# Ten places instead of five for the row sums of layer 1's shift and scale in a two-layer diffusion step

## The chip, the core and the metric

The kernel runs on one core of a Trainium2 chip. Five engines work side by side, each through its own queue in order: TensorE (PE) multiplies matrices, VectorE (DVE), ScalarE (ACT) and GpSimd (POOL) work on elements, SyncE (SP) starts transfers. An instruction that needs another engine's result waits, and everything behind it on its engine waits too. The metric is the device time of one execution in microseconds (us).

## What is computed

The reference is one step of a two-layer trunk over 512 latent and 128 context tokens of width 1024. Layer 0 is gated attention with 16 query heads in 4 groups, layer 1 a gated linear recurrence. In front of each layer the tokens are scaled and shifted by two vectors that come from a condition vector:

```python
def _adaln(cond, w, b):
    mod = jax.nn.silu(cond.astype(jnp.float32)) @ w.astype(jnp.float32) + b.astype(jnp.float32)
    mod = mod.astype(cond.dtype)
    return jnp.split(mod, 3, axis=-1)
...
for i in range(DEPTH):
    sh_p, sc_p, g_p = _adaln(c_ctx, ada_w[i], ada_b[i])
    sh_s, sc_s, g_s = _adaln(c, ada_w[i], ada_b[i])
    hp = xp * (1.0 + sc_p) + sh_p
    hs = xs * (1.0 + sc_s) + sh_s
    # layer 0: attention over 640 keys (latent) or 128 keys (context); layer 1: recurrence
    xp = _layer_norm(DEEPNORM_ALPHA * xp + g_p * out_p, ln_gain[i], ln_bias[i])
    xs = _layer_norm(DEEPNORM_ALPHA * xs + g_s * out_s, ln_gain[i], ln_bias[i])
```

Layer 1's shift and scale (sh and sc for i = 1) are needed only when layer 0 is done, and are worked out while its attention runs.

## The kernel before

**Attention and side work.** Layer 0's attention is a main thread of steps (`att_gen`), one tuple of steps for each of 32 sample units and 4 prompt units. A sample unit is one head with 256 queries. Its steps are two fronts (scores `sc` on PE, row maximum `nm` on DVE, exponential `p` on ACT, reciprocal `rc` on DVE, scaling of `p` on POOL), three transpositions (`pt` on PE, copied to `pts` by ACT, or by DVE for the short last one) and, for each pair of units, the product with the values (`pot` on PE) that DVE multiplies into `gs`. The scores use two PSUM double banks in turn.

A side thread (`Side`) is stepped between the attention's steps. It holds, in this order: the query chunks 1, 2 and 3 (`q_gen`), the splitting of the output weights `attn_w_out` (`wo_gen`: ACT casts to `wohi`, DVE subtracts to `wolo`) and the splitting of `gs` into `hhi` (ACT) and `hlo` (POOL). The string `SIDE_AT` says how many side steps follow each attention step. Where a front of query chunk c is due, `side.until` runs whatever is left of that chunk on the spot.

**A query chunk.** `q_gen` multiplies 640 tokens by 256 columns in three units of 2, 2 and 1 token tiles, 24 products (`qmm`) a tile in two steps of 12. After a unit come sums of squares (`sq`, `ss`), rotation (`u`, `r`), scaling (`qn`), the split (`qs`) and transpositions (`qps`) into `X`, which the scores read. Between those steps `q_gen` takes one step of a filler at the places that `FILL_AT` names: a digit for the unit's first tile, a letter for the step (a to d are the product steps, e stands behind the rotation). Whatever of the filler is left by the chunk's end runs there, one step after another. For chunks 1 and 2 the filler works out gate vectors on PE.

**The row sums.** For chunk 3 the filler is `cols_gen`: five jobs, each a 128x1024 piece of layer 1's weights (`in_ada_c`, 512 KB, loaded by SP into one of three `raw` buffers). A job has two row sums, one for each condition vector: DVE multiplies the piece by the vector (`silb`, spread over all partitions) and adds up along the row, with the products themselves written to a throwaway tile `spill` (line 361). The trace shows each as one SCALAR_TENSOR_TENSOR and one DVE_READ_ACCUMULATOR. So there are ten filler steps. Behind the last, DVE adds the bias (`shsc`, line 365), from which `modA` and `modB` are made (lines 1144 to 1146), and POOL issues two transfers of layer 0's gate into the buffer that held `silb` (line 341). The other 11 of the 16 jobs ran earlier.

**What sets the order.** The first half of the program, up to the end of attention, is written in the order of these steps and then reordered by a scheduler with a model of each engine's time (`tc.block(schedule_with_timeline_sim=True)`); instructions that are pinned keep their order among themselves. The second half follows its own plan and is not touched.

Of the kernel before, what the change touches and what calls it, by code (L numbers as in the profile page):

```python
# [34 lines left out]
HALVES = ((0, 320), (320, 640))  # L35
HALF_PIECES = (slice(0, 512), slice(512, 1024))
RAW_AHEAD = 2
FILL_AT = {1: '0b0e2e', 2: '0b0e2e4e', 3: '0a0b0e2e4e'}
LEAD = (1, 1)
RAW_START = 8  # L40
EARLY = 2
# [3 lines left out]
SIDE_T = 2.2  # L45
SIDE_AT = (
    "0100021120010100020100012001210201010101000002111001021000000130"
    "2002020010001200011201020101300010100102000000201112120001100001"
    "3100002000111000000310010102010113001000012000120300210000012")
RES_AT = 6  # L50
SEVEN = range(1, RH - 1)
# [103 lines left out]
def hybrid_step(ctx: ExitStack, tc: tile.TileContext, a: dict, o: dict):  # L155
# [589 lines left out]
    def q_gen(c, X, fill):  # L745

        w = Weights("attn_w_in", c, (nc.vector, nc.vector), tuple(last_split))
        yield
        spots = {FILL_AT[c][i:i + 2] for i in range(0, len(FILL_AT[c]), 2)}
        pend = None  # L750
# [1338 lines left out]
```

## Time and profile before

| | us |
|---|---|
| median of three runs | 818.72 |
| lowest, highest | 817.18, 822.82 |
| the profiled execution, its own time | 818.12 |
| its span, first to last instruction | 816.3 |
| granted TensorE clock, mean | 0.993 |
| query chunk 3's products on PE | 233 to 269 |
| end of attention, start of the output product | 324.5 |

Times inside the span are counted from its start. A row of the chain of waits gives start, length, engine, tile and line of a piece of the path that ended last. A row of the timeline gives start, length, engine, line and operation, and in square brackets how long the engine had stood idle and for whom. Where instructions of an engine are pipelined, their lengths overlap, and the distance between starts is what one costs.

### The profile page before, as it was taken

To read this page: it belongs to the slowest core of one execution; us is meant where nothing else is said; L and a number is where in the kernel's file an instruction comes from. 1 tells how busy PE (TensorE), PEld (TensorE's weight loads), DVE (VectorE), ACT (ScalarE), POOL (GpSimd) and SP (SyncE) were. 2 spreads that over 40 slices of the span, in tenths; PEclk is the share of its full clock that TensorE was granted. 3 is DMA by queue.
4 is the path that set the end of the run, shared out by engine and by line. 5 is a ranking of instruction groups with operands and counts; after the bars stand their busy time and mean duration, and the time that the engine had idled before them with its cause. 6 is when DMAs were issued, how large, how long until landed. Compare 5 with 4: busy or idle time off the path is not lost.

```text
span 816.3 us, 19278 instructions
## 1 busy us (share of the span) xinstructions
PE 791.5 (97%) x7953; PEld 700.9 (86%) x7953; DVE 598.5 (73%) x1083; ACT 451.3 (55%) x894; POOL 217.1 (27%) x261
## 2 busy tenths in 40 slices
PE   8999999999999989999999999999999999999994
PEld 6779999878888766888999999998999999998873
DVE  4567767686578885676799777868786876788376
ACT  2252545566565786232565766747484856667342
POOL 0124001353434853010600224122140414131211
PEclk9999999999999999999999999999999999999998
DMA  9944343224140060631531342325242344232442
GB/s 325 395 160 159 104 155 132 104 96 165 52 130 28 27 206 7 238 118 49 143 105 53 98 120 71 111 64 128 66 122 85 98 108 144 92 106 74 142 149 77
DMA packets 36630, 98.12 MB, mean 120 GB/s; under 512 B 5296, under 2 KB 12480, under 8 KB 36544
## 3 DMA queue, kind: packets, MB, share of 16 engines
q1 hardware_dynamic: 25872, 78.95, 28.9%
q0 software_dynamic: 4768, 14.18, 6.0%
q10 hardware_dynamic: 5904, 3.78, 1.5%
q8 instruction: 62, 1.02, 0.5%
q14 instruction: 24, 0.20, 0.1%
HBM read 86.06 MB, written 10.83 MB: 119 GB/s over the span
## 4 chain that ended last, share of the span: by engine, by line
PE 82%; DVE 8%; ACT 4%; DMA 2%; issue 2%; POOL 2%; SPq 0%; ACTq 0%; DVEq 0%; POOLq 0%
PE vgps L1383 8%; PE vgps L1379 4%; PE pot L950 4%; PE pt L1036 4%; PE rps L1451 4%; PE outp L1213 3%; PE outp L1215 3%; PE outp L1214 3%; PE rps L1405 3%; PE rps L1407 3%; PE rps L1453 3%; PE rps L1406 3%; PE rps L1452 3%; PE acc L568 3%; PE sc L923 2%; PE lv L1682 2%
## 5 line engine op out<-in xcount | busy, mean ns | idle before, releaser
L1029 POOL TENSOR_SCALAR p<-p,rc 128x640 f32<-128x640 f32 x64 | 57.1, 898 | 114.8 <-DVE rc L1028 97.6
L1720 POOL COPY At<-near 32x160 f32<-32x160 f32 x32 | 15.6, 489 | 197.0 <-PE lv L1688 196.0
L1023 ACT ACTIVATE p<-sc,nm 128x640 f32<-128x640 f32 x64 | 51.2, 802 | 24.9 <-DVE nm L1018 15.7
L1018 DVE TENSOR_REDUCE nm<-sc 128x1 f32<-128x640 f32 x64 | 51.7, 816 | 13.0 <-PE sc L924 12.8
L1405 PE MATMUL rps<-h1hi,rw 128*128 128x320 f32 x176 | 55.4, 315 | 0.0
L1407 PE MATMUL rps<-h1hi,rw 128*128 128x320 f32 x176 | 54.5, 310 | 0.1
L1406 PE MATMUL rps<-h1lo,rw 128*128 128x320 f32 x176 | 54.4, 309 | 0.0
L1036 PE MATMUL pt<-small,p 128*128 128x128 f32 x320 | 49.0, 277 | 2.8 <-DVE pts L928 1.2
L1383 PE MATMUL vgps<-rw,h1hi 128*128 128x512 f32 x180 | 48.3, 393 | 0.0
L1036 PEld LDWEIGHTS pt<-small,p 128*128 128x128 f32 x320 | 36.5, 140 | 11.6 <-issue 5.7
L1655 ACT COPY kc<-A 128x640 f32<-128x640 f32 x48 | 38.3, 797 | 12.2 <-DVE A L1706 11.5
L928 ACT COPY pts<-pt 128x512 f32<-128x512 f32 x64 | 36.1, 590 | 15.3 <-PE pt L1036 15.2
L923 PE MATMUL sc<-kk,X 128*128 128x320 f32 x128 | 42.3, 340 | 1.7 <-ACT p L1023 1.6
L1726 ACT COPY At<-lv 32x160 f32<-32x160 f32 (+1 forms) x48 | 15.9, 330 | 45.9 <-PE lv L1688 45.5
L950 PE MATMUL pot<-pts,vv 128*64 128x256 f32 x320 | 38.3, 384 | 2.1 <-DVE pts L928 2.0
L380 PE MATMUL gps<-hhi,whi 128*128 128x320 f32 x128 | 40.0, 312 | 0.1
L381 PE MATMUL gps<-hlo,whi 128*128 128x320 f32 x128 | 39.6, 309 | 0.0
L382 PE MATMUL gps<-hhi,wlo 128*128 128x320 f32 x128 | 39.5, 309 | 0.0
L1383 PEld LDWEIGHTS vgps<-rw,h1hi 128*128 128x128 f32 x180 | 33.1, 188 | 6.7
L924 PE MATMUL sc<-klo,X 128*128 128x320 f32 x128 | 38.5, 310 | 0.0
L1383 PE MATMUL vgps<-wspare,h1hi 128*128 128x512 f32 x140 | 38.2, 394 | 0.0
L1711 DVE TENSOR_TENSOR A<-A,T 128x640 f32<-128x640 f32 x32 | 27.2, 850 | 10.9 <-PE lv L1682 10.8
(347 smaller groups left out, 2633.9 us busy)
## 6 DMA issues: line engine op xcount, KB each, us to landing
raw<-in_rec_w_in SPq DMA_DIRECT2D x40, 512.0 KB, 3.7
raw<-in_ada_m SPq DMA_DIRECT2D x16, 512.0 KB, 8.1
raw<-in_attn_w_in SPq DMA_DIRECT2D x16, 512.0 KB, 5.2
raw<-in_ada_s SPq DMA_DIRECT2D x16, 512.0 KB, 3.7
adaraw<-in_ada_c SPq DMA_DIRECT2D x11, 512.0 KB, 5.5
raw<-in_attn_w_out SPq DMA_DIRECT2D x8, 512.0 KB, 3.8
raw<-in_rec_w_out SPq DMA_DIRECT2D x8, 512.0 KB, 3.6
raw<-in_ada_c SPq DMA_DIRECT2D x5, 512.0 KB, 4.4
```

What stands on the lines that cost most here:

```text
L380: nc.tensor.matmul(ps[:, :320], w.hi(k)[:, c], hhi[:, k, t], start=(k == 0), stop=False)
L381: nc.tensor.matmul(ps[:, :320], w.hi(k)[:, c], hlo[:, k, t], start=False, stop=False)
L923: nc.tensor.matmul(out, X[:, h, t0:t0 + P], kk[:, c, k0:k1], start=True, stop=False)
L950: nc.tensor.matmul(pot[j * HD:(j + 1) * HD, :CW], vv[:, slot, c * HD:(c + 1) * HD], moving[j], start=first, stop=last)
L1018: nc.vector.tensor_reduce(nm[:, 0:1], sc[:, :, :320], AX.XY, ALU.max, negate=True)
L1023: return nc.scalar.activation(halves(p[:]), sc[:, :, :320], AF.Exp, bias=nm[:, 0:1], accum_out=su[:, 0:1])
L1029: nc.gpsimd.tensor_scalar(p, p, rs[:, 0:1], 1.0, ALU.mult, ALU.mult)
L1036: nc.tensor.transpose(pt[:, i * 256 + q * P:i * 256 + (q + 1) * P], ps[q][:, (k0 + i) * P:(k0 + i + 1) * P], ident)
L1383: nc.tensor.matmul(out, h1hi[:, k, t], wvg[i][:, k % 4].rearrange("p e n -> p (e n)"), start=(k == 0), stop=(k == KT - 1))
L1405: nc.tensor.matmul(ps[:, j, :320], hi[:, k, :], h1hi[:, k, t], start=(k == 0), stop=False)
L1406: nc.tensor.matmul(ps[:, j, :320], hi[:, k, :], h1lo[:, k, t], start=False, stop=False)
L1407: nc.tensor.matmul(ps[:, j, :320], lo[:, k, :], h1hi[:, k, t], start=False, stop=(k == KT - 1))
```

## The change

Two constants. `FILL_AT` names ten places in chunk 3 instead of five: behind three of the first unit's four product steps, three of the second's four, one of the third's two, and, as before, behind the rotation of each of the three units. `SIDE_AT` gets six more side steps, in the attention steps in which the chunk's products stand, so that the products keep about their place although there are more steps among them.

```diff
-FILL_AT = {1: '0b0e2e', 2: '0b0e2e4e', 3: '0a0b0e2e4e'}
+FILL_AT = {1: '0b0e2e', 2: '0b0e2e4e', 3: '0a0b0c0e2a2b2d2e4a4e'}
...
 SIDE_AT = (
     "0100021120010100020100012001210201010101000002111001021000000130"
-    "2002020010001200011201020101300010100102000000201112120001100001"
+    "2002020010001200011201020101301010110102010010201112120101101001"
     "3100002000111000000310010102010113001000012000120300210000012")
```

In written order, before, row sums 1 to 3 stand in the first unit, 4 after the second, 5 after the third, and 6 to 10 at the end of the chunk; 7 to 10, with the chunk's last transposition behind them, run in one go where `side.until` forces the rest out. Now 1 to 4 stand in the first unit, 5 to 8 in the second and 9 and 10 in the third, nothing is forced out, and the first split of `attn_w_out` comes three attention steps earlier. No instruction is added or removed on any engine. SP issues the same transfers in the same order.

The scheduler then makes of it the following. DVE, around the rotation of chunk 3's first unit (`r`, `qn`, `qs`), before:

```order
L673 TENSOR_TENSOR qn<-r,rstd 128x512
L955 TENSOR_TENSOR gs<-pot,gs 128x256
L928 COPY pts<-pt 128x256
L361 SCALAR_TENSOR_TENSOR spill,shsc_80<-raw,silb 128x1024
L1028 RECIPROCAL rc<-su 128x1
L976 TENSOR_REDUCE nmp<-pscp 128x4
L726 TENSOR_TENSOR qs_3169<-qn,qs_3169 128x8x64
```

One row sum, the fourth, stood here. Now, on DVE at the same place:

```order
L955 TENSOR_TENSOR gs<-pot,gs 128x256
L673 TENSOR_TENSOR qn<-r,rstd 128x512
L361 SCALAR_TENSOR_TENSOR spill,shsc_80<-raw,silb 128x1024
L928 COPY pts<-pt 128x256
L726 TENSOR_TENSOR qs_3153<-qn,qs_3153 128x8x64
L361 SCALAR_TENSOR_TENSOR spill,shsc_80<-raw,silb 128x1024 x2
L1018 TENSOR_REDUCE nm<-sc 128x1
L928 COPY pts<-pt 128x256
L361 SCALAR_TENSOR_TENSOR spill,shsc_80<-raw,silb 128x1024
L1028 RECIPROCAL rc<-su 128x1
L976 TENSOR_REDUCE nmp<-pscp 128x4
```

Four row sums, the fifth to the eighth, stand here with four short operations between them; the fourth has moved ahead of this place.

DVE at the end of chunk 3, where the last split `qs` and the splits of the output weights `wolo` stand, before:

```order
L361 SCALAR_TENSOR_TENSOR spill,shsc_80<-raw,silb 128x1024
L928 COPY pts<-pt 128x256
L1018 TENSOR_REDUCE nm<-sc 128x1
L726 TENSOR_TENSOR qs_3551<-qn,qs_3551 128x4x64
L361 SCALAR_TENSOR_TENSOR spill,shsc_80<-raw,silb 128x1024
L1028 RECIPROCAL rc<-su 128x1 x2
L361 SCALAR_TENSOR_TENSOR spill,shsc_80<-raw,silb 128x1024
L1018 TENSOR_REDUCE nm<-sc 128x1
L361 SCALAR_TENSOR_TENSOR spill,shsc_80<-raw,silb 128x1024 x2
L1018 TENSOR_REDUCE nm<-sc 128x1
```

Five row sums, the last of the ten. Now, on DVE around the last split:

```order
L673 TENSOR_TENSOR qn<-r,rstd 128x256
L1018 TENSOR_REDUCE nm<-sc 128x1
L1028 RECIPROCAL rc<-su 128x1
L726 TENSOR_TENSOR qs_3565<-qn,qs_3565 128x4x64
L1018 TENSOR_REDUCE nm<-sc 128x1
L1028 RECIPROCAL rc<-su 128x1
L928 COPY pts<-pt 128x256
L1018 TENSOR_REDUCE nm<-sc 128x1
L264 TENSOR_TENSOR wolo<-raw,wohi 128x1024 x2
```

None is left there; the bias and `modA`, `modB` have gone with them to a place ahead of the third unit's rotation.

POOL, from the splitting of `gs` on, before:

```order
L1161 TENSOR_TENSOR hlo<-gs,hhi 128x640 x4
L213 TENSOR_TENSOR rstd<-rs_t,mhalf 128x4
L1029 TENSOR_SCALAR p<-p,rc 128x640 x3
L1161 TENSOR_TENSOR hlo<-gs,hhi 128x640
L1029 TENSOR_SCALAR p<-p,rc 128x640 x3
L341 DMA gate_3606<-gated_102 128x1024 x2
L1029 TENSOR_SCALAR p<-p,rc 128x640 x6
```

The two gate transfers stood behind ten scalings and splits. Now, on POOL:

```order
L1161 TENSOR_TENSOR hlo<-gs,hhi 128x640 x3
L341 DMA gate_3571<-gated_102 128x1024
L1029 TENSOR_SCALAR p<-p,rc 128x640
L341 DMA gate_3571<-gated_102 128x1024
L1161 TENSOR_TENSOR hlo<-gs,hhi 128x640
L1029 TENSOR_SCALAR p<-p,rc 128x640
L213 TENSOR_TENSOR rstd<-rs_t,mhalf 128x4
```

They are issued among the first splits, one by one, ahead of the scalings that they stood behind.

## The prediction

> **What bounds the kernel now.** I read the page first: how long the span is and which engine fills it.
>
> ```profile
> span 816.3 us, 19278 instructions
> PE 791.5 (97%) x7953; PEld 700.9 (86%) x7953; DVE 598.5 (73%) x1083; ACT 451.3 (55%) x894; POOL 217.1 (27%) x261
> ```
>
> TensorE is busy 97% of the span and the change takes no product away. So only time in which PE stands or runs below its pace can be won. The change touches the attention from about 228 to 324.5 us, so I cut that into stretches (columns: length, then busy time and count of PE, PEld, DVE, ACT, POOL, then granted clock, DMA share, GB/s).
>
> ```profile
> 228.00:278.15 50.15, 49.33 (x410) 42.89 (x409) 38.30 (x82) 34.18 (x77) 26.54 (x28) 1.00 0.21 64
> 278.15:295.14 16.99, 12.23 (x88) 9.17 (x86) 16.97 (x34) 12.73 (x27) 12.15 (x10) 1.00 0.51 160
> 295.14:324.50 29.36, 28.05 (x219) 20.66 (x219) 18.66 (x40) 20.75 (x49) 12.14 (x14) 1.00 0.21 70
> ```
>
> In the second stretch PE falls to 12.23 of 16.99 us, and DVE is busy for 16.97: DVE is the bound there, and nowhere else nearby. The chain of waits says with what (start, length, engine, tile, line):
>
> ```profile
> 276.30 1.24 PE pt L1036 x10
> ...
> 279.07 1.20 DVE spill L361
> ...
> 285.74 1.06 DVE spill L361
> 286.82 1.74 DVE spill L361 x3
> ...
> 291.20 0.64 DVE wolo L264
> ...
> 295.14 0.98 PE pt L1036 x7
> ```
>
> The path leaves PE behind 276.30 and is back at 295.14. Between, it runs through row sums and what stood behind them on DVE. How much of the stretch is lost? Its PE work, grouped, and what the same instructions cost where PE runs without waits:
>
> ```profile
> L1036 PE MATMUL pt<-small,p 128*128 128x128 f32 x40 | 6.5, 280 | 2.5 <-DVE pts L928 1.2 <-POOL p L1029 0.7 <-ACT pts L928 0.5
> L923 PE MATMUL sc<-kk,X 128*128 128x320 f32 x12 | 4.2, 356 | 0.8 <-ACT p L1023 0.8
> L924 PE MATMUL sc<-klo,X 128*128 128x320 f32 x12 | 3.6, 308 | 0.0
> L950 PE MATMUL pot<-pts,vv 128*64 128x256 f32 x20 | 2.4, 384 | 1.5 <-DVE pts L928 1.5
> L734 PE MATMUL qps<-identr,qs 128*128 128x128 f32 x4 | 0.5, 238 | 0.0
> ```
> ```profile
> 230.06 0.87 PE pt L1036 x8
> 234.25 0.12 PE qmm L391
> 297.87 2.31 PE pot L950 x20
> 300.77 0.15 PE sc L923
> 300.92 0.14 PE sc L924
> ```
>
> A transposition costs 0.87/8 = 0.109 us, a score 0.145, twenty value products 2.31. The stretch's work is 44 x 0.109 + 24 x 0.145 + 2.31 = 10.6 us. It took 16.99, so 6.4 us are lost: the most that this change can win here.
>
> **The change part by part: what leaves the end of the chunk.** Five row sums leave the stretch, with the bias and the two modulation vectors.
>
> ```profile
> L361 DVE SCALAR_TENSOR_TENSOR spill<-raw,silb 128x1024 f32<-128x1024 f32 x5 | 7.2, 1458 | 0.0
> L365 DVE TENSOR_TENSOR shsc<-shsc,small 128x16 f32<-128x16 f32 x1 | 0.6, 594 | 0.0
> L1029 POOL TENSOR_SCALAR p<-p,rc 128x640 f32<-128x640 f32 x7 | 9.0, 1289 | 3.4 <-DVE modB L1146 3.4
> L341 POOL DMA_DIRECT2D gate<-gated x2 | 1.2, 602 | 1.4 <-DVE spill L361 1.4
> L1023 ACT ACTIVATE p<-sc,nm 128x640 f32<-128x640 f32 x7 | 5.6, 801 | 2.0 <-DVE nm L1018 1.1 <-DVE rc L1028 0.9
> L736 ACT CAST X<-qps 128x512 fp32r<-128x512 f32 x1 | 0.6, 587 | 1.8 <-PE qps L734 1.8
> ```
>
> DVE drops from 16.97 by 7.2 + 0.6 and about 0.8 of small ones to some 8.4 us, below PE's 10.6. POOL loses the 1.4 us wait for the last row sum and its scalings should fall back from 1289 ns towards the 859 of the rows below: 12.15 - 7 x 0.43 - 1.2 = 8 us. What is late next is ACT: 12.73 us of work that stays (exponentials, copies, the casts of the output weights). If it works without a gap, the stretch takes 12.7 us and the gain is 16.99 - 12.73 = 4.3. The ends: at PE's pace, with ACT's surplus worked off in the next stretch (20.75 of 29.36 us busy), 6.4; if only the 2.0 us that ACT idles for DVE (1.1 and 0.9) come back, 2.0. I take 4.3, the row of the engine that is next.
>
> **What arrives among the products.** In this place the first stretch's rows price the work:
>
> ```profile
> L361 DVE SCALAR_TENSOR_TENSOR spill<-raw,silb 128x1024 f32<-128x1024 f32 x5 | 6.0, 1218 | 1.2 <-DMA raw<-in_ada_c 1.2
> L1018 DVE TENSOR_REDUCE nm<-sc 128x1 f32<-128x640 f32 x17 | 13.7, 818 | 5.5 <-PE sc L924 5.4
> L928 DVE COPY pts<-pt 128x256 f32<-128x256 f32 x9 | 3.8, 417 | 1.2 <-PE pt L1036 1.2
> L673 DVE TENSOR_TENSOR qn<-r,rstd 128x512 f32<-128x512 f32 x2 | 1.8, 892 | 0.1
> L1029 POOL TENSOR_SCALAR p<-p,rc 128x640 f32<-128x640 f32 x16 | 13.6, 859 | 18.5 <-DVE rc L1028 13.0 <-PE pt L1036 5.0 <-PE pot L950 0.4
> 247.90 2.38 PE L950 MATMUL pot<-pts,vv 128*64 128x256 f32 x20
> 251.59 0.41 DVE L955 TENSOR_TENSOR gs<-pot,gs 128x256 f32<-128x256 f32 x1
> 254.06 0.92 DVE L726 TENSOR_TENSOR qs<-qn,qs 128x512 fp32r<-128x512 f32 x1
> 246.69 0.41 PE L923 MATMUL sc<-kk,X 128*128 128x320 f32 x1 [0.68 <-ACT p L1023]
> ```
>
> DVE's load rises from 38.3 to about 38.3 + 5 x 1.3 + 1.1 = 45.9 of 50.15 us: it fits, barely. Row sums 5 to 8 stand in a bunch there, so I count from the end of one value product to the next. DVE: gs 0.41, qn 0.89, a row sum 1.22 and its read 0.08, pts 0.42, qs 0.92, two row sums 2.60, nm 0.82, pts 0.42 = 7.8 us, and this second `pts` is what the next value product waits for. PE has 48 products, 20 transpositions, 4 long scores and 8 short ones in between: 48 x 0.12 + 20 x 0.109 + 4 x 0.145 + 8 x 0.109 = 9.4 us. That cover leaves 1.6. But DVE was late there already: pot ended at 250.28, gs began at 251.59, so 1.3 is gone and 0.3 remains. The scaling behind the fourth row sum is due 2.4 us later than it is ready by the same count. So the cost is between 0 and, should all four row sums lie on the path, 4 x 1.30 = 5.2. The nearest row of a wait here is PE's 0.68 for a score that stood behind DVE and ACT; I take one such, 0.7, because the count comes out near zero.
>
> **Costed at nothing.** Row sums 9 and 10 stand in front of the third unit's products, and 4 moves up by one row sum's length; without cover each would cost 1.3. The transfers of the pieces keep their order on SP; a piece needs a buffer that an earlier row sum freed, and these now come earlier, so I expect no wait longer than the 1.2 that stands in the row above. The loads of the output weights start earlier for the same reason. POOL's two gate issues (1.2 us) move ahead of scalings, but behind splits that POOL does anyway. The first `wohi` and `wolo` come three attention steps earlier; DVE has room there now. Behind 324.5 the program is the same, only shifted.
>
> Sum: -4.3 + 0.7 = -3.6 us. The profiled execution took 818.1 (span 816.3 and 1.8 around it), which gives 814.5; it lies 0.6 under the median of 818.7, against which I forecast **815.1**.
>
> **A rule weighed.** POOL's scaling took 1289 ns on average where five row sums ran and 859 where they were rarer; a row sum took 1458 against 1218. Stretching thus adds 0.24 to a row sum. The Trainium skill, SBUF — State Buffer, "Who interferes with whom", says that a VectorE instruction with two SBUF inputs contends with a GpSimd one that reads SBUF, through a port that both share; a row sum is such an instruction. The trace agrees with the direction. By its exclusive form, where the loser waits for the other's whole instruction, each of four could wait up to 0.86 for a scaling, 3.4 together, which makes the last rival below the dearer one: the sum would be -0.9.
>
> **The rivals.**
> *Half comes back.* The row sums go, but ACT keeps its waits for others: X waited 1.8 us for PE. Then 2.0 return less 0.7: 817.4. For it: ACT's row names DVE for only 2.0. Against: qps itself stood behind DVE's late qs.
> *PE's full pace.* All 6.4 return and the bunch is free: 812.3. Against: ACT's 12.73 is more than 10.6.
> *The bunch decides; the row sums do not lie one by one.* The scheduler has put four of them between two value products. From 0.3 us of further lateness on, each microsecond of DVE is one of PE. With row sums as in the crowded row, 3 x 0.24 = 0.7 more, it costs 0.4, which I have covered; with all four on the path, 5.2 against 4.3: 819.6, slower than before. Against: 48 products as cover, and PE's order holds them there.
>
> **How the numbers follow.** The forecast, 813.5 to 816.5, gets 0.58; half, up to 819, 0.20; full pace 0.10; the bunch 0.12. The range runs from full pace to the bunch, 812.0 to 820.0, rounded outward, and leaves under 2 in 10 outside. About 1%, 8.2 us, is what a measurement of this kernel can tell from no change. The whole loss is 6.4, so faster by over 1% gets 0.02; slower by over 1% would need more than every moved row sum on the path: 0.02; within 1% 0.96.
>
> **What would show it.** Right: DVE's share in the stretch behind the last products falls to about two thirds, no spill in the chain there, PE's share back above nine tenths, the attention ends near 321. Wrong: waits of the value product or of transpositions for `pts` and `rc` around 250 to 262, row sums over 1.5 us there, or ACT with idle time for PE in the old place.

## The result, and the profile after

The changed kernel took 824.98 us (median of 8 runs, 822.61 to 826.87) beside 819.06 us for the kernel before (8 runs, 817.18 to 822.82). The ratio is 1.0064, with a 95% interval of 1.0048 to 1.0081: slower by some 5.3 us by the ratio, where 3.6 us less was forecast. The profiled execution took 826.87 us, the slowest of the eight, while that of the kernel before, at 818.12, lies below its median; the parts read below therefore hold more loss than 5.3 us. Its page begins:

```profile
span 825.1 us, 19288 instructions
PE 793.6 (96%) x7953; PEld 701.5 (85%) x7953; DVE 605.8 (73%) x1083; ACT 450.2 (55%) x894; POOL 215.1 (26%) x261
```

The first question is in which part of the program the time came. The instructions of one tile, grouped by line, give the first and the last start of each line. Two of these rows enclose the attention: its first score product, and the first product of the output projection behind it. The kernel before, and then the changed one:

```profile
L923 PE MATMUL sc<-kk,X x128: 302/309/417, 130.8 to 316.1; 128*128 128x320 f32 x128
L1213 PE MATMUL outp<-wohi,hhi x80: 389/389/504, 324.6 to 382.7; 128*128 128x512 f32 x80
```
```profile
L923 PE MATMUL sc<-kk,X x128: 302/310/636, 131.4 to 323.6; 128*128 128x320 f32 x128
L1213 PE MATMUL outp<-wohi,hhi x80: 388/390/502, 332.9 to 391.1; 128*128 128x512 f32 x80
```

From first score to output projection it was 324.6 - 130.8 = 193.8 us, and it is now 332.9 - 131.4 = 201.5. Behind it 816.3 - 324.6 = 491.7 us were left, and now 825.1 - 332.9 = 492.2. So the loss lies inside the attention. Nor is it spread out there (columns as in the prediction's windows):

```profile
248.00:256.00 8.00, 8.00 (x70) 7.21 (x66) 7.96 (x18) 3.06 (x7) 4.76 (x3) 1.00 0.03 10
256.00:264.00 8.00, 8.00 (x70) 6.86 (x69) 7.43 (x15) 5.40 (x16) 3.75 (x3) 1.00 0.36 124
264.00:272.00 8.00, 7.64 (x63) 6.15 (x61) 7.97 (x14) 7.32 (x16) 4.28 (x3) 1.00 0.17 52
272.00:280.00 8.00, 2.79 (x20) 2.30 (x20) 7.93 (x10) 0.59 (x1) 7.35 (x8) 0.90 0.39 145
280.00:288.00 8.00, 6.90 (x32) 5.55 (x31) 4.20 (x11) 5.60 (x12) 4.42 (x5) 0.67 0.00 0
288.00:296.00 8.00, 7.15 (x59) 5.61 (x58) 6.81 (x14) 7.72 (x17) 2.96 (x4) 1.00 0.17 44
```

Through the four row sums that stand close together (248 to 264) TensorE's line shows no idle time, and in the stretch of the old burst (288 to 296) it is busy for 7.15 of 8 us where it had 5.06 before, though by then the changed kernel is some 7 us behind and at other work. But from 272 to 280 us it works only 2.79 us, and behind that the granted clock is 0.67. TensorE's waits in 262 to 300 us, the two largest groups (total, number, longest), and the chain of waits (start, length, what) say what it waited for:

```profile
PE qps L734 <- DVE r L657: 5.2, 1, 5.2
PE sc L923 <- ACT p L1023: 1.9, 2, 1.1
```
```profile
269.69 1.36 DVE shsc L365
...
271.07 1.48 DVE modA L1144
272.55 1.53 DVE modB L1145
...
274.11 3.52 DVE modB L1146
277.63 0.07 DVE rc L1028
...
278.06 0.57 DVE rs_t L212
278.63 0.33 DVE r L657
...
279.09 0.72 PE qps L734 x4
```

The four smallest operations that the change moved, the bias and the three that make `modA` and `modB`, all on 128x16 numbers, fill VectorE for 277.63 - 269.69 = 7.9 us. In the kernel before the three at lines 1144 to 1146 took 0.16, 0.16 and 0.15 us, and the bias 0.59. The first of the three there:

```profile
292.33 0.16 DVE L1144 TENSOR_TENSOR modA<-shsc,lnc 128x16 f32<-128x16 f32 x1
```

In the changed kernel, behind the four in VectorE's order waits `r`, whose reading frees the PSUM bank that `qps` needs. What GpSimd does in that time, by its timeline:

```profile
268.50 5.54 POOL L1161 TENSOR_TENSOR hlo<-gs,hhi 128x640 fp32r<-128x640 f32 x3
273.99 0.66 POOL L341 DMA_DIRECT2D gate<-gated  x1
274.69 0.80 POOL L1029 TENSOR_SCALAR p<-p,rc 128x640 f32<-128x640 f32 x1
275.44 0.59 POOL L341 DMA_DIRECT2D gate<-gated  x1
276.05 1.54 POOL L1161 TENSOR_TENSOR hlo<-gs,hhi 128x640 fp32r<-128x640 f32 x1
```

GpSimd's line has no gap, and the last `modB` ends (277.63) with the `hlo` that ends at 276.05 + 1.54 = 277.59. The first three take about 1.5 us each, which is the median length of an `hlo` in this kernel (1.555 us). From this I made **theory A**: VectorE's operations with two inputs in SBUF are held while GpSimd works, however small they are. Its rivals: **B**, the bunch of row sums costs the time; **C**, the small operations are slow in themselves, because each waits for the result of the one before.

How much of the loss is the wait, and how much the clock? The finer windows:

```profile
276.00:280.00 4.00, 0.91 (x6) 0.82 (x8) 3.97 (x8) 0.00 (x0) 3.39 (x4) 0.80 0.63 228
280.00:284.00 4.00, 4.00 (x18) 3.12 (x16) 2.12 (x6) 3.53 (x8) 1.28 (x2) 0.50 0.00 0
284.00:288.00 4.00, 2.90 (x16) 2.43 (x16) 2.08 (x5) 2.07 (x5) 3.15 (x4) 0.85 0.00 0
```

TensorE stood still for 5.2 us and ran at down to half its clock afterwards: in 276 to 288 us the granted clock lacks 0.20, 0.50 and 0.15. Times the busy time that is 0.2 + 2.0 + 0.4 = 2.6 us of pace, by an estimate from these rows. Together 7.8, against 7.7 us by which the attention grew. What the old stretch saved is in the 7.7 as well, so smaller waits, which I did not add up, make up for it.

### The profile page after: what moved, and what is told of

Read it like the earlier page. It is cut to its first block, busy times and chain, and to the rows that moved or that the text cites. A ratio compares the mean times of both kernels' runs of the same rounds, so it can differ in the third digit from the quotient of the medians.

```text
span 825.1 us, 19288 instructions
## 1 busy us (share of the span) xinstructions
PE 793.6 (96%) x7953; PEld 701.5 (85%) x7953; DVE 605.8 (73%) x1083; ACT 450.2 (55%) x894; POOL 215.1 (26%) x261
## 4 chain that ended last, share of the span: by engine, by line
PE 81%; DVE 9%; ACT 3%; DMA 3%; issue 2%; POOL 1%; SPq 0%; DVEq 0%; ACTq 0%; POOLq 0%
PE vgps L1383 8%; PE vgps L1379 4%; PE outp L1213 4%; PE pot L950 4%; PE outp L1215 4%; PE outp L1214 4%; PE pt L1036 4%; PE rps L1451 4%; PE rps L1405 3%; PE rps L1407 3%; PE rps L1406 3%; PE rps L1453 3%; PE rps L1452 3%; PE sc L923 2%; PE lv L1682 2%
```

## The experiments

The ratios are to the kernel before, timed in the same batch on the same chip; its medians there were 820.2 to 821.1 us. A profile's whole span also holds a difference from ahead of the attention, which the edits leave alone: the first score starts anywhere from 129.8 to 133.9 us. So each profile is also read by the length of the attention, first score to first `outp` product, which was 193.8 before and 201.5 after. Each kernel was profiled once, so how much this length varies between executions of one kernel is not measured.

| kernel | median us | ratio, 95% interval | attention, us |
|---|---|---|---|
| 1 changed, four small operations late | 823.37 | 1.0034 [1.0016, 1.0051] | 198.2 |
| 2 before, four small operations late | 819.62 | 0.9988 [0.9973, 1.0003] | 194.5 |
| 3 before + four two-input adds | 822.25 | 1.0030 [1.0013, 1.0047] | 195.3 |
| 4 before + four one-input reductions | 819.90 | 0.9999 [0.9984, 1.0014] | 193.8 |
| 5 changed, `hlo` late | 818.93 | 0.9981 [0.9966, 0.9996] | 192.7 |
| 6 before, `hlo` late | 819.68 | 0.9989 [0.9973, 1.0005] | 193.4 |
| 7 changed, both late | 818.15 | 0.9973 [0.9959, 0.9987] | 192.7 |
| 8 row sums' table alone | 826.01 | 1.0069 [1.0047, 1.0090] | 200.7 |
| 9 side steps' table alone | 823.08 | 1.0032 [1.0016, 1.0047] | 196.2 |
| 10 changed + useless transpositions | 825.27 | 1.0062 [1.0044, 1.0080] | 197.7 |
| 11 as 7, three `hlo` on VectorE | 820.00 | 0.9998 [0.9981, 1.0015] | 194.9 |
| 12 changed, gate transfers on SyncE | 821.80 | 1.0016 [0.9993, 1.0038] | 199.5 |

**1 and 2: the four small operations leave their place.** In both kernels they are issued behind the last multiplication of the attention; the order of everything else stays.

```diff
-        if ft == KT - 1:
+        if ft == KT - 1 and s == 0:
...
-    modA, modB = h1_mod()
+    with tc.issue_after(last_av[0].ins):
+        nc.vector.tensor_tensor(shsc[1][:, 1], shsc[1][:, 1], view(adab, 4 * KT, [[1, KT], [0, 2]]), ALU.add)
+        modA, modB = h1_mod()
```

> The changed kernel with one thing moved: the bias add of the row sums and the three small operations that make modA and modB (four 128x16 operations on VectorE) stand behind the last multiplication of the attention instead of among GpSimd's splits of gs. The order of every other instruction is the changed kernel's. Theory A, held by GpSimd: in the changed kernel these four took 1.40, 1.48, 1.60 and 3.52 us because each waited for GpSimd instructions that were running; TensorE then stood 5.2 us and ran 6.3 us at half clock, 8.3 us in all. Moved to a place where GpSimd is idle they take under 0.3 us each, and the time falls by 5 to 9 us, to 816 to 820. Theory B, the bunch: the row sums among the products made VectorE late and the small operations only stand where the lateness shows; the time stays within 2 us of 825. Theory C, slow in themselves: the four wait for each other's results and take 1.4 to 3.5 us at the new place too, where the output product waits for VectorE; 823 to 830.

> The kernel before with the same four small operations moved behind the attention, row sums where they were. They took 0.59, 0.16, 0.16 and 0.15 us there. Theory A: GpSimd was held up by row sums or idle beside them, so little is won: 0 to 1.5 us, 817.5 to 819. Theory B: the same, 0 to 1 us. Theory C: they were fast in the kernel before, so no effect of their own; 817.5 to 820. It is the base for the first run: the difference of the two is what the moved row sums alone do, with the small operations out of the way.

The kernel before does not feel the move. The changed one wins back a part only, from 1.0064 to 1.0034. The profile of the first shows why. At their new place the four take 0.17 us each, but VectorE's next operation with two SBUF inputs is held instead, 3.25 us for a `qn` that takes 0.42 us in kernel 5; VectorE's row, then GpSimd's rows beside it:

```profile
278.80 3.25 DVE L673 TENSOR_TENSOR qn<-r,rstd 128x256 f32<-128x256 f32 x1
```
```profile
277.91 1.57 POOL L1029 TENSOR_SCALAR p<-p,rc 128x640 f32<-128x640 f32 x2
279.45 1.54 POOL L1161 TENSOR_TENSOR hlo<-gs,hhi 128x640 fp32r<-128x640 f32 x1
280.98 1.73 POOL L1029 TENSOR_SCALAR p<-p,rc 128x640 f32<-128x640 f32 x2
```

Behind it TensorE waits 2.4 us, and in 284 to 288 us its clock is 0.50. So it is not something in the four operations (against C, by their 0.17 us), but the size that I expected of A was missed: 823.37 us lies in the ranges of B and C. What decides between A and B are kernels 3 to 7.

**3 and 4: the same place in the kernel before, with two inputs or with one.** Four extra operations that nobody reads are placed among the `hlo`, ahead of the last unit's rotation; the added work is no part of the result.

```diff
+            if c == 3 and tt0 == TS:
+                t16 = tiny.tile([P, 16], F32, tag="t16", name="t16", bufs=1)
+                for _ in range(4):
+                    tc.keep_in_program_order(nc.vector.tensor_tensor(t16, small[:, 130:146], small[:, 146:162], ALU.add))
...
+                    tc.keep_in_program_order(nc.vector.tensor_reduce(t16[:, 0:1], small[:, 130:146], AX.X, ALU.add))
```

> The kernel before with four extra 128x16 additions on VectorE, both inputs in SBUF, results unused, ahead of the rotation of chunk 3's last unit, where GpSimd splits gs for 6 us. Theory A: each takes 1 to 2 us for 0.16 us of work, VectorE falls 4 to 6 us behind, the time rises by 2 to 6 us, to 821 to 825. Theory B and C: independent of each other, they take under 0.2 us each; the time stays within 1 us of 819.

> As the run with four extra additions, at the same place, but each extra operation is a sum over 16 columns, with one input in SBUF. Theory A in the form that only an operation with two SBUF inputs is held: under 0.2 us each, the time within 1 us of 819. If any VectorE operation on SBUF is held by GpSimd there: 1 to 2 us each and 821 to 825. Theory B and C: under 0.2 us, within 1 us of 819.

VectorE's timeline, first with the adds, then with the reductions and the operation ahead of them, and last what GpSimd does beside the reductions:

```profile
274.12 1.61 DVE L770 TENSOR_TENSOR t<-small 128x16 f32<-128x16 f32 x1
275.65 0.15 DVE L1028 RECIPROCAL rc<-su 128x1 f32<-128x1 f32 x1
275.76 1.90 DVE L770 TENSOR_TENSOR t<-small 128x16 f32<-128x16 f32 x3
```
```profile
271.09 0.78 DVE L212 TENSOR_SCALAR rs_t<-ss 128x4 f32<-128x4 f32 x1
271.79 0.16 DVE L770 TENSOR_REDUCE t<-small 128x1 f32<-128x16 f32 x1
271.87 0.15 DVE L1028 RECIPROCAL rc<-su 128x1 f32<-128x1 f32 x1
271.98 0.58 DVE L770 TENSOR_REDUCE t<-small 128x1 f32<-128x16 f32 x3
```
```profile
268.76 6.12 POOL L1161 TENSOR_TENSOR hlo<-gs,hhi 128x640 fp32r<-128x640 f32 x4
```

The same 16 numbers cost 1.61 + 1.90 = 3.5 us when added to 16 others and 0.16 + 0.58 = 0.7 when summed, and the kernel is slower with the first and not with the second. Two of the four adds were held and two took 0.18 us, where I had expected all four. That shows A's hold of additions with two inputs in a kernel that doesn't have the change. The Trainium skill, SBUF — State Buffer, "Who interferes with whom", has this condition: a VectorE instruction with two SBUF inputs contends with a GpSimd one that reads SBUF, and a reduction never does on this chip. The trace agrees with both halves. But two inputs are not the whole condition: `rs_t` (line 212), ahead of the reductions, has a single tensor in SBUF as its input and took 0.78 us beside the `hlo`, against 0.16 where GpSimd is idle. In kernel 9 it took 1.43 us and in kernel 12 1.08, and both times it ended within 0.03 us of an `hlo`. So what kernels 3 and 4 tell apart is an addition and a sum, not every operation by the number of its inputs.

**5, 6 and 7: GpSimd's splits leave instead.** The six `hlo` are held in the written order behind the scalings, in the changed kernel, in the one before, and in the changed one together with the edit of 1.

```diff
+        with tc.issue_after(last_scale[0]) if eng is nc.gpsimd else ExitStack():
+            (eng or nc.vector).tensor_tensor(dst_lo, src, dst_hi.bitcast(F32), ALU.subtract)
-        (eng or nc.vector).tensor_tensor(dst_lo, src, dst_hi.bitcast(F32), ALU.subtract)
```

> The changed kernel with GpSimd's six splits of gs (hlo) held in written order behind the scalings of p, so that they run some 25 us later; the four small VectorE operations stay where the change put them. In the first run, with the four moved away, another operation with two SBUF inputs (qn of the last unit) took 3.25 us behind hlo and two scalings, TensorE waited 2.4 us and fell to half clock again. Theory A, held by GpSimd: without hlo in this place the four small operations and qn take under 1 us each, TensorE does not stand for more than 1.5 us nor fall to half clock there, and the gain of the moved row sums shows: 814 to 818. Theory B, the bunch of row sums makes VectorE late: no better than the first run, 822 to 825. A new loss where hlo now stands is the rival to A: then waits of over 1 us by VectorE behind hlo after 290 us, and 818 to 822.

> The kernel before with the six hlo held back in the same way, row sums where they were. Theory A: the five row sums at the end of the chunk still fill VectorE, only their stretching by GpSimd (1458 instead of 1218 ns) goes, 1 to 1.5 us: 817 to 819.5. Theory B: no effect, 818.5 to 820.5. It is the base for the run before.

> The changed kernel with both: hlo held back and the four small operations behind the attention. Theory A: within 1 us of the run with hlo alone held back, since without hlo the four cost little, or faster by up to 1: 813 to 818. Theory B: 822 to 825.

With `hlo` away and the small operations where the change put them, the loss is gone: 1.0064 becomes 0.9981, no wait of TensorE in the attention from 228 us on reaches 1.4 us, and the clock stays at 1.00. VectorE's order is the changed kernel's up to `r`; behind that the scheduler orders anew. The first and the last of the four in VectorE's timeline of the fifth kernel:

```profile
271.29 0.17 DVE L365 TENSOR_TENSOR shsc<-shsc,small 128x16 f32<-128x16 f32 x1
...
271.79 0.17 DVE L1146 TENSOR_TENSOR modB<-modB,shsc 128x16 f32<-128x16 f32 x1
```

They took 0.17 to 0.18 us each, with the bunch of row sums ahead of them as in the changed kernel: against B, which had 822 to 825 for both, and C. A's own ranges were just missed, 818.93 against 814 to 818 and 818.15 against 813 to 818, and the sixth, 819.68, lies in B's range and just above A's: what was left to win was over-sized. The fifth and the seventh beat both kernels: their intervals lie below 1. The seventh, 818.15, is the fastest that I found. What `hlo` costs now lies later; a new loss there was the rival written down for the fifth, with 818 to 822. A window of the seventh:

```profile
304.00:312.00 8.00, 6.67 (x46) 4.62 (x45) 4.57 (x11) 5.51 (x14) 8.00 (x8) 1.00 0.00 1
```

GpSimd is full there, and TensorE lacks 1.33 us; the sixth kernel has the same 6.67.

**8 and 9: each of the two tables alone.**

```diff
-FILL_AT = {1: '0b0e2e', 2: '0b0e2e4e', 3: '0a0b0e2e4e'}
+FILL_AT = {1: '0b0e2e', 2: '0b0e2e4e', 3: '0a0b0c0e2a2b2d2e4a4e'}
...
-    "2002020010001200011201020101300010100102000000201112120001100001"
+    "2002020010001200011201020101301010110102010010201112120101101001"
```

> Half of the change: ten places for the row sums, but the old side steps. In the order that comes out, the four small operations and both gate transfers stand ahead of all six hlo. Theory A: the four are fast (under 0.6 us each), so the loss of the changed kernel shrinks to what qn or others wait for behind hlo: 816 to 822. Theory B: the same bunching of row sums, so as slow as the changed kernel: 823 to 827. If the six more side steps were the harm: 815 to 819.

> The table of side steps alone, with the old five places for row sums. The bias and the three modulation products keep their place behind the last row sums, 25 rows further on in VectorE's order than in the changed kernel and behind four of the six hlo splits. Theory A (two-input operations held by GpSimd): as before, 818 to 821, with the four small operations under 0.7 us each. Rival B (the moved steps themselves cost): 823 to 826. If A and the run with the row sums' table alone (826.0) both hold, the whole loss belongs to that one table.

Both are slower, and theory A missed both numbers, which fell where its rivals had them (826.01 in B's 823 to 827, 823.08 in the moved steps' 823 to 826): I had gone by the order, in which the four operations stand ahead of the splits (8) or behind most of them (9). With the row sums' table alone the four operations met the splits on the chip all the same. VectorE, then GpSimd:

```profile
271.44 0.63 DVE L365 TENSOR_TENSOR shsc<-shsc,small 128x16 f32<-128x16 f32 x1
272.10 6.99 DVE L1144 TENSOR_TENSOR modA<-shsc,lnc 128x16 f32<-128x16 f32 x1
```
```profile
271.00 1.20 POOL L341 DMA_DIRECT2D gate<-gated  x2
272.24 0.81 POOL L1029 TENSOR_SCALAR p<-p,rc 128x640 f32<-128x640 f32 x1
273.00 6.05 POOL L1161 TENSOR_TENSOR hlo<-gs,hhi 128x640 fp32r<-128x640 f32 x4
```

One `modA` is held through a scaling and four splits, 6.99 us, until GpSimd has nothing more to do; the two operations behind it take 0.16 and 0.17 us. So B's number came about by A's mechanism. With the side steps' table alone the small operations are not there, but a row sum, which has two SBUF inputs as well, took 2.53 us beside an `hlo` and a scaling, where its neighbours took 1.21; a wait of TensorE of 1.49 us follows. That fits A's mechanism, but that it is all of the ninth kernel's 1.0032 is not shown; the moved side steps may cost something of their own.

**10: TensorE kept busy in its wait.** One transposition, the last that TensorE does ahead of the wait, is done 29 times.

```diff
-                for q in range(2):
+                for q in (0,) * (28 if (c, h, qh, k0, i) == (2, 2, 0, 0, 0) else 0) + (0, 1):
```

> The changed kernel with one transposition of pt, the one that TensorE runs just before its 5.2 us wait, done 29 times instead of once (28 x 0.11 = 3.1 us of work without use). The scheduler then orders what follows differently, so only the stretch to 285 us is compared, not the whole time. If the lower granted clock comes from TensorE standing still: the clock stays at 1.00 through 280 to 285 and a score product in the chain costs 0.15 instead of 0.27 us, while the small operations are held as before (modB over 3 us). If the clock falls for another reason, 0.50 stays. Time between 818 and 826.

TensorE's timeline and its windows:

```profile
274.65 3.33 PE L1036 MATMUL pt<-small,p 128*128 128x128 f32 x29
```
```profile
276.00:280.00 4.00, 4.00 (x37) 3.45 (x35) 2.75 (x7) 2.51 (x7) 3.97 (x5) 1.00 0.72 264
280.00:284.00 4.00, 2.74 (x17) 1.99 (x16) 3.66 (x8) 3.69 (x9) 3.99 (x5) 1.00 0.01 2
```

The clock stays at 1.00 where it was 0.50 in the changed kernel, and no wait of TensorE from 228 us to the end of the attention is longer than 1.2 us. So the low clock came from standing still. Three of the four small operations were held here too (1.40, 1.47, 0.17 and 1.43 us), but none for more than one split, so that part of the expectation missed. The time as a whole, 825.27, says nothing: 3 us of it are the useless work, and the order behind differs.

**11: three of the late splits on VectorE.**

```diff
-            split_act(hhi[:, k, :], hlo[:, k, :], gs[:, k, :], nc.gpsimd if k < 6 else nc.vector)
+            split_act(hhi[:, k, :], hlo[:, k, :], gs[:, k, :], nc.gpsimd if k in (0, 2, 4) else nc.vector)
```

> The version with both moved late (818.15), but three of the six late hlo splits on VectorE instead of GpSimd. If GpSimd, which is full from 300 to 312 us, is what is left of the loss there (TensorE busy 2.67 of 4 in 308 to 312): 816.8 to 817.8. If VectorE, which then has three more two-input operations of 1.1 us or more, takes over: 818 to 820, and these splits last over 1.5 us beside GpSimd's scalings.

It is no better than before: 0.9998. In 304 to 312 us TensorE gets back to 7.81 of 8, as hoped, and the three splits on VectorE take 0.80 to 0.82 us, not over 1.5. But behind that stands a new wait of 1.69 us for a scaling, with shorter ones on both sides of it, and the clock falls at the very end of the attention, to 0.57 in 324 to 328 us. Over a longer stretch it reads:

```profile
320.00:345.00 25.00, 21.93 (x102) 16.69 (x102) 13.96 (x23) 9.31 (x13) 1.97 (x3) 0.93 0.48 165
```

**12: the two gate transfers on another queue.** The longest hold of the changed kernel began within a gate issue, and that of kernel 8 too.

```diff
-        gate_load(0, nc.gpsimd)
+        gate_load(0, nc.sync)
```

> The changed kernel with the two gate transfers issued on SyncE instead of GpSimd; the order on every engine is the same up to this place, and differs in a few rows behind it. The second modB was held 3.52 us from within the first gate issue (273.99 to 274.65) to the end of the next hlo. If the gate issues are what makes a hold last over several GpSimd instructions: no small operation is held over 1.6 us, TensorE waits for r under 3.4 us, the clock stays at 1.00, 818 to 821. If they are not: one of the four is held for 2.3 us or more again (a scaling and a split), and the time stays at 822 to 826.

The last `modB` is held for 0.73 us instead of 3.52, and no small operation for more than 1.6:

```profile
273.05 1.59 DVE L1145 TENSOR_TENSOR modB<-shsc,lnc 128x16 f32<-128x16 f32 x1
274.68 0.73 DVE L1146 TENSOR_TENSOR modB<-modB,shsc 128x16 f32<-128x16 f32 x1
```

The median falls to 821.80, between the two ranges that I had expected, and the interval holds 1. The clock's part of the expectation missed: the profiled execution, at 825.97 the slowest of this kernel, still has a wait of 2.9 us and a clock of 0.62 and 0.52 in 276 to 284 us. It is not typical: of the ten executions two, this one and one of 825.64, have a mean granted clock of 0.987, and the other eight, at 0.990 to 0.996, took 819.84 to 823.02. So moving the gate issues makes the kernel faster, but this profile, with its attention of 199.5 us, does not show by what; on SyncE they also stand ahead of four loads of the output weights, and what that does is not tested apart. That the gate issues make a hold long is not shown either: the long holds of the changed kernel and of kernel 8 began within one, but the `qn` of kernel 1 was held 3.25 us with none beside it, and in kernel 10, with the gate issues behind the third `hlo` as in the changed kernel, no small operation was held for more than 1.47 us. What decides whether GpSimd lets VectorE in between two of its instructions stays open.

## Why the prediction was wrong, point by point

**What bounds the kernel** was read rightly: behind the attention nothing changed, and TensorE's waits for VectorE are what the time hangs on.

**The step that failed** is the pricing of the four small operations. The prediction took "the bias and the two modulation vectors" out of the old stretch as 0.6 and about 0.8 us of relief, put them as 1.1 us into VectorE's load at the new place, "it fits, barely", and charged nothing on the path. The new place is among GpSimd's splits. There, in the profiled execution, they took 7.9 us, TensorE stood for 5.2 and lost about 2.6 more to the clock, by the estimate above. Kernel 5 shows it by taking GpSimd's splits away from the place, kernels 3 and 4 by additions and sums at the same place in the kernel before, kernel 10 for the clock.

**The gate issues**, "behind splits that POOL does anyway", were not free. The order of GpSimd's rows, shown ahead of the prediction, had them between two splits. With them on SyncE the ratio falls from 1.0064 to 1.0016, and the two intervals do not meet. By what mechanism they cost this stays open, as said under 12.

**The rule weighed** was the right rule at the wrong instructions. It was applied to row sums against scalings, at most 0.86 us each. The prediction itself says that the loser waits for the other's whole instruction; by that the length of VectorE's operation doesn't matter, so the 128x16 ones had to be charged a split of 1.5 us each, 6 us for four. That the wait could even span several instructions, 3.52 and 6.99 us, goes beyond the rule. The row sums, to which the rule was applied, were held little in the changed kernel: 1.40 us at most against a median of 1.216.

**The gain of 4.3** was over-sized. The cleanest pair is 5 against 6, which differ in the two tables alone and start the attention within 0.1 us of each other. In the place of the old burst TensorE's share did come back, in kernel 6 and then in kernel 5:

```profile
288.00:296.00 8.00, 5.49 (x38) 4.37 (x37) 8.00 (x16) 7.68 (x15) 3.78 (x6) 1.00 0.84 268
```
```profile
288.00:296.00 8.00, 7.70 (x57) 5.96 (x58) 5.58 (x13) 6.19 (x13) 3.73 (x5) 1.00 0.40 137
```

From 280 to 296 us that is 15.55 us of TensorE's work against 13.19, 2.4 more. But kernel 5 has 0.7 less in 264 to 280 (15.13 against 15.86) and 0.6 less in 296 to 320 (21.64 against 22.25). By the medians the pair gives 0.9981 / 0.9989 = 0.9992, by the attention's length 0.7 us; the two intervals overlap, so the gain of the tables alone is not shown. Kernel 7, which also has the four operations late, stands some 1.3 us below kernel 6 by the ratios (0.9973 / 0.9989 = 0.9984), and these intervals overlap too. Part of the old loss was GpSimd's as well: over 32 us around the old burst TensorE is busy for 27.24 us in the kernel before and for 29.19 in kernel 6, whose attention starts 2.6 us later (272 to 304 and 274.6 to 306.6 us); the median hardly moved, 0.9989.

**The bunch of row sums, 0.7**, was not too small. TensorE was busy for all of 248 to 264 us in the changed kernel. The lateness behind it is seen better in kernel 5, where nothing is held: there TensorE is busy for 0.7 us less than in kernel 6 in 264 to 280 us, and that is all that the bunch, row sums 9 and 10 (costed at nothing) and the moved side steps can have cost in this stretch together. The rival that ended on the slow side was right in its sign, and named the wrong place.

**What would show it:** the attention ends at 332.9, not near 321. Of the signs named for a failure none appeared: no wait around 250 to 262 us, no row sum over 1.5 us there (1.21 to 1.23), and ScalarE waited only 0.3 us for TensorE in 278 to 296. I had looked for trouble only where the prediction saw work being added, not where it saw 1 us of small change. The loss, 0.64%, is also smaller than the 1% that the prediction called what can be told from no change, yet its interval, 0.48 to 0.81%, lies clear of zero.

## What to carry to other kernels

When a new order moves VectorE's work, look at what GpSimd does at the new place, and price each operation there that has two SBUF inputs by the length of GpSimd's instructions, not by its own. What avoided it here was GpSimd's work moved away (kernel 5), and in kernel 4 a sum in place of an addition; one SBUF input alone was not enough for `rs_t`. A wait that leaves TensorE without work for some microseconds can be charged twice, once as the wait and once as the low clock behind it. And in single profiles a part that is enclosed by two of TensorE's own products leaves out what differs ahead of it, here up to 4 us at the first score.

## What the hardware showed that was not expected

An addition of 16 numbers per partition, 0.17 us when GpSimd is idle, was held for 3.52 us and a multiplication for 6.99, through several of GpSimd's instructions in a row, although three others in the same place were let in after one. With the gate transfers issued elsewhere the longest of the four took 1.59 us; with TensorE's wait filled, the gate issues in place, 1.47. And an operation with a single SBUF tensor, `rs_t`, took up to 1.43 us beside an `hlo`, where it takes 0.16 with GpSimd idle.

The clock fell to about half after single waits of 5.2 us (changed kernel and kernel 8) and 2.9 us (kernel 12), after one of 2.43 us with 1.14 and 0.63 us shortly ahead of it (kernel 1), and in kernel 11 where 0.33, 1.69 and 0.52 us of waiting stood close together; not in the kernel before, whose longest wait in this stretch was 1.53 us, nor in kernel 4 with 1.61. The Trainium skill, TensorE: Matmul & The Clock Gate, "HAM oscillation — how this bites in real kernels", puts the bound at gaps of more than some 3.4 us. The 5.2 us agree with it; the waits of kernels 12, 1 and 11 are shorter and were followed by a low clock too.
